# Twelve taps of a depthwise convolution as diagonal products, its taps shared anew among four engines, and three output blocks queued behind a norm's mean

## The chip, the cores and the metric

The kernel runs on one core of one Trainium2 chip. The metric is the device time of one execution in microseconds (us). All times on a trace count from the start of the span. Engines are named as on the profile: PE is TensorE's matmuls, PEld its weight loads, DVE is VectorE, ACT ScalarE, POOL GpSimd, SP the queue that issues the DMAs.

## The reference

An encoder of two layers over 512 tokens of width 1024 in float32. The change lies in the mixer of the second layer, which has two branches over one input projection `p = h @ cd_w_in`, then one output projection and a residual:

```
y_c = real(fftn(p[:, :512] in 4 groups of 128 channels, over tokens and channels, ortho))
val, gate = split(p[:, 512:])
u   = val * sigmoid(gate)                               # 512 channels
u   = depthwise_conv(u, conv_w (31 taps), conv_b)       # centred, per channel
y_d = silu(layernorm(u) * ln_g + ln_b)                  # over the 512 channels
x   = x + gate_vector * (concat([y_c, y_d]) @ cd_w_out)
```

Behind it stand an RMS norm with scale and shift, and a gated feed-forward part.

## The kernel before, in words

Activations lie transposed: 128 channels on the partitions, 512 tokens along the row, so 1024 channels are 8 blocks of 128x512. A projection is done block by block (`gemm`): each fp32 weight block is split into a rounded part `whi` (ScalarE, L136) and a rest `wlo` (VectorE, L137), each input into `h` and its rest, and three products of type fp32r (L142 to L144) make one fp32 product. Norm sums and the channel transform of the Fourier branch use plain fp32 products.

The order of each engine's queue is set by a scheduler that ranks instructions by the place in the program and by priorities (`tc.high_priority`); it is fixed when the program is built. Each engine works its queue in that order.

`layer1` is the mixer. It makes eight blocks for the convolution branch (`hps`, 15 zeros on either side), then four for the Fourier branch:

- `channels(u)`: ScalarE copies the block from PSUM to `u` (L1077); VectorE adds and subtracts the block and its mirror image, the halves `eo` (L1042); TensorE multiplies these with the channel table (L1046, tile `m`), ScalarE and VectorE split the result (`vh`, `vl`, L1049, L1050).
- `tokens(g, v)`: TensorE multiplies with the sequence tables, twelve products of 258 columns (tiles `g` and `c`); VectorE puts the two results together into `y` (L1068, L1069), which is split (L161, L162) as input of the output projection.

The convolution has 31 taps for each of four blocks. Block b's taps from `FO[b]` on go to GpSimd (multiplied by ScalarE into a ring of eight `ta` tiles, L1103, and added by GpSimd into `cpa`, L1108), those below to VectorE, one fused multiply and add each into a PSUM bank (`h`, L1114), after a first one by ScalarE (L1111). FO is {0: 6, 1: 31, 2: 22, 3: 2}: 57 taps on VectorE, 63 on GpSimd (60 of them multiplied by ScalarE). L1117 adds the two sums. Then the layer norm: TensorE sums the four accumulators with a matrix of ones (tile `pm`, L1124), VectorE subtracts the mean (L1127), ScalarE squares (L1129), TensorE sums the squares (`pv`, L1130), ScalarE takes logarithm and exponential (L188, L189), VectorE multiplies (L1134), ScalarE applies silu (L1135).

The output projection (`out_proj`) has two halves: part 0 multiplies the four Fourier blocks with half the rows of `cd_w_out` and adds to the residual `x` (L386), part 1 does so with the four convolution blocks. All eight output blocks of part 0 stand ahead of the convolution in the program.

## Time and profile before

| | |
|---|---|
| median of 3 runs | 1523.39 us (1521.78 to 1528.9) |
| profiled execution, own time | 1523.8 us |
| its span | 1522.0 us |
| busy on PE, DVE, ACT, POOL | 1404.5, 1036.9, 688.2, 162.9 us |
| mean granted TensorE clock | 0.944 of full speed |

A busy TensorE is not TensorE at its peak, since matmuls are pipelined; a stretch is read by its waits and by the granted clock. The clock has two levels, 1.2 and 2.4 GHz, shown as 0.5 and 1.0. The mixer of the second layer begins near 980 us with the modulation of its input; its output projection ends at 1144.92 us.

### The profile page before, as it was taken

Reading aid. Unit: us, or ns where it says so; the run is one execution under the profiler, and the core shown is the slowest. Engines: PE = TensorE matmul, PEld = TensorE weight load, DVE = VectorE, ACT = ScalarE, POOL = GpSimd, SP = SyncE. Lnnn points to the kernel's source line nnn. Section 1 sums busy time; section 2 is a strip of 40 time slices with the busy share of each in tenths; the row PEclk is TensorE's granted clock in tenths of the full one; section 3 lists DMA queues with packets and bytes.
Section 4 is the critical chain, followed back from the end, with each engine's and each line's share of the span. In section 5 each row is a group of like instructions: output and inputs, shape, how many; then the busy total and the mean of one; then the engine's idle time right before and its main releaser. Section 6 shows DMA issues by size and latency. Waiting matters only on the chain.

```text
span 1522.0 us, 22368 instructions
## 1 busy us (share of the span) xinstructions
PE 1404.5 (92%) x8422; PEld 1113.8 (73%) x8422; DVE 1036.9 (68%) x2121; ACT 688.2 (45%) x1231; POOL 162.9 (11%) x226
## 2 busy tenths in 40 slices
PE   5988889889998996999999999998979999999997
PEld 3765567666666674788888888886758888888886
DVE  7689876888696864766565784679968654544544
ACT  4455454635545442643233243576555432332343
POOL 1030210102010000000000000069700000000000
PEclk8998789989999996999999999999799999999999
DMA  9221123412243532344544873221123332223221
GB/s 373 85 78 41 47 54 89 133 46 79 85 149 97 186 108 97 109 154 162 184 140 139 280 268 88 98 91 56 49 70 125 111 97 97 94 87 111 94 73 56
DMA packets 76572, 174.29 MB, mean 115 GB/s; under 512 B 28208, under 2 KB 34224, under 8 KB 75440
## 3 DMA queue, kind: packets, MB, share of 16 engines
q1 hardware_dynamic: 76464, 172.87, 35.0%
q8 instruction: 66, 1.08, 0.3%
q14 instruction: 42, 0.34, 0.1%
HBM read 166.02 MB, written 6.82 MB: 114 GB/s over the span
## 4 chain that ended last, share of the span: by engine, by line
PE 75%; DVE 10%; ACT 5%; issue 4%; DMA 3%; POOL 2%; SPq 1%; DVEq 0%; ACTq 0%; POOLq 0%
PE g L142 9%; PE g L144 9%; PE g L143 9%; PE c L142 5%; PE c L143 5%; PE c L144 5%; PE o L142 3%; PE o L144 3%; PE o L143 3%; PE h L144 3%; PE h L143 3%; PE h L142 3%; DVE wlo L137 2%; PE c L731 2%; PE m L613 2%
## 5 line engine op out<-in xcount | busy, mean ns | idle before, releaser
L136 ACT CAST whi<-raw 128x512 fp32r<-128x512 f32 (+1 forms) x402 | 242.3, 608 | 514.0 <-PE g L143 201.9
L137 DVE TENSOR_TENSOR wlo<-raw,whi 128x512 fp32r<-128x512 f32 (+1 forms) x402 | 279.3, 699 | 180.9 <-ACT whi L136 177.5
L142 PE MATMUL g<-h,whi 128*128 128x512 f32 x586 | 240.7, 411 | 14.9 <-ACT h L170 5.2
L144 PE MATMUL g<-h,wlo 128*128 128x512 f32 x586 | 235.4, 402 | 4.4 <-DVE wlo L137 4.4
L143 PE MATMUL g<-h,whi 128*128 128x512 f32 x586 | 236.3, 403 | 2.9 <-DVE h L171 2.9
L142 PEld LDWEIGHTS g<-h,whi 128*128 128x128 f32 x586 | 113.6, 194 | 45.1 <-ACT h L170 6.5
L144 PEld LDWEIGHTS g<-h,wlo 128*128 128x128 f32 x586 | 113.2, 193 | 31.9 <-DVE wlo L137 5.9
L143 PEld LDWEIGHTS g<-h,whi 128*128 128x128 f32 x586 | 113.4, 193 | 28.7 <-DVE h L171 4.1
L142 PE MATMUL c<-h,whi 128*128 128x512 f32 x306 | 121.8, 398 | 4.8 <-ACT h L161 4.8
L143 PE MATMUL c<-h,whi 128*128 128x512 f32 x306 | 121.4, 397 | 0.0
L144 PE MATMUL c<-h,wlo 128*128 128x512 f32 x306 | 121.1, 396 | 0.0
L1108 POOL TENSOR_TENSOR cpa<-cpa,ta 128x512 f32<-128x512 f32 x60 | 87.2, 1465 | 3.2
L142 PEld LDWEIGHTS c<-h,whi 128*128 128x128 f32 x306 | 58.8, 192 | 18.4 <-ACT h L161 5.6
L639 DVE TENSOR_TENSOR tt<-L,xi 128x60 f32<-128x60 f32 (+24 forms) x248 | 56.2, 227 | 21.1 <-DMA L<-nd 15.6
L230 DVE SCALAR_TENSOR_TENSOR ra<-ra,row 128x1024 f32<-128x1024 f32 x56 | 68.0, 1218 | 0.8 <-DMA ra<-ada 0.7
L143 PEld LDWEIGHTS c<-h,whi 128*128 128x128 f32 x306 | 58.9, 192 | 12.0
L144 PEld LDWEIGHTS c<-h,wlo 128*128 128x128 f32 x306 | 58.7, 192 | 12.1
L641 DVE TENSOR_TENSOR xi<-xi,tt 128x60 f32<-128x60 f32 (+24 forms) x248 | 54.4, 219 | 5.4
L1020 POOL MEMSET hp<- 128x15 f32 x4 | 0.4, 112 | 471.9 <-DVE nt L312 471.9
L142 PE MATMUL o<-h,whi 128*128 128x512 f32 x122 | 48.1, 394 | 0.8 <-DVE ot L791 0.8
L1189 POOL TENSOR_TENSOR h<-x,rs 128x256 f32<-128x256 f32 x4 | 3.7, 934 | 416.2 <-ACT rs L301 416.2
L1103 ACT ACTIVATE ta<-hp,cols 128x512 f32<-128x512 f32 x60 | 41.9, 720 | 13.4 <-POOL cpa L1108 12.8
(431 smaller groups left out, 2974.3 us busy)
## 6 DMA issues: line engine op xcount, KB each, us to landing
raw<-ffn_up SPq DMA_DIRECT2D x88, 512.0 KB, 3.4
ra<-ada SPq DMA_DIRECT2D x56, 512.0 KB, 4.1
raw<-ab_in SPq DMA_DIRECT2D x35, 512.0 KB, 3.6
raw<-ffn_down SPq DMA_DIRECT2D x32, 448.0 KB, 3.3
raw<-ada SPq DMA_DIRECT2D x24, 512.0 KB, 4.1
ada<-ada SPq DMA_DIRECT2D x8, 1024.0 KB, 10.7
raw<-ffn_down SPq DMA_DIRECT2D x16, 512.0 KB, 3.5
raw<-cd_in SPq DMA_DIRECT2D x12, 512.0 KB, 3.3
```

The source lines that it names most:

```text
L136: act.copy(hi[:, :n, :], raw[:, k0:k0 + n, :])
L137: dve.tensor_tensor(lo[:, :n, :], raw[:, k0:k0 + n, :], hi[:, :n, :].bitcast(F32), op=ALU.subtract)
L142: pe.matmul(ps, whi, xhi, start=first, stop=False)
L143: pe.matmul(ps, whi, xlo, start=False, stop=False)
L144: pe.matmul(ps, wlo, xhi, start=False, stop=last)
L230: dve.scalar_tensor_tensor(w, w, 1.0, row, op0=ALU.mult, op1=ALU.mult, accum_out=dst)
L613: pe.matmul(ps[hr, c, :], at[hr, c0 + c], ibk[hr, c0 + c].rearrange("p s t -> p (s t)"), start=True, stop=True)
L639: dve.tensor_tensor(tv, Lv[:, j + 1:, j:j + 1].broadcast_to([P, n, m]), xi[:, j:j + 1, :m].broadcast_to([P, n, m]), op=ALU.mult)
L641: dve.tensor_tensor(xi[:, j + 1:, :m], xi[:, j + 1:, :m], tv, op=ALU.add)
L731: pe.matmul(ps[h][:, c, :], W[hr, c0 + c, :], BRS[hr, c0 + c, :], start=True, stop=True)
L1103: act.activation(tp, hps[b][:, i:i + T], AF.Copy, scale=col("dconv_w", i * 4 + b))
L1108: pl.tensor_tensor(pa, pa, tp, op=ALU.add)
```

## The change

Five things change, all in `layer1`:

1. FO becomes {0: 6, 1: 31, 2: 17, 3: 16}. GpSimd has 54 operations (51 taps from ScalarE), VectorE 55 taps.
2. The first twelve taps of block 3 become twelve fp32 products on TensorE into bank `o`: the weights are a diagonal matrix with the tap's 128 coefficients, the moving operand is the shifted row. The diagonals are new data (`dconv_dg`), loaded in three DMAs of 256 KB into two tiles `dg`. The bias of block 3 goes in with its first `ta` tile.
3. `channels` reads one operand of each half `eo` from the PSUM bank; the other still comes from the copy `u`.
4. Output blocks 5 to 7 of part 0 are issued behind the last product of the norm's mean (`pm`); the norm gets a high priority (`FIRM`). The norm sums block 2 last.
5. The accumulators are the tiles `ys[4:]`, and silu works in place.

```diff
-FO = {0: 6, 1: 31, 2: 22, 3: 2}
+FO = {0: 6, 1: 31, 2: 17, 3: 16}
+PT = {3: 12}
...
-    def out_proj(x, y, src, mod, part, norm=None):
-        for o in range(KB if norm is None else norm.nfull):
+    def out_proj(x, y, src, mod, part, norm=None, os=None):
+        for o in os or range(norm.nfull):
...
-                dve.tensor_tensor(eo[:, i], u[:, 1:H + 1], u[:, T - 1:H - 1:-1], op=op)
+                dve.tensor_tensor(eo[:, i], pu[:, 1:H + 1], u[:, T - 1:H - 1:-1], op=op)
...
-        out_proj(x, yy, "cd_out", mods[1, 0][0], 0)
-        accs = []
-        for b in range(4):
-            accs.append(mk(lp, [P, T], f"acc{b}"))
+        out_proj(x, yy, "cd_out", mods[1, 0][0], 0, os=range(5))
+        accs = ys[4:]
...
+                if i == first + 1 and b in PT:
+                    act.activation(tp, hps[b][:, i:i + T], AF.Identity, scale=col("dconv_w", i * 4 + b),
+                                   bias=col("dconv_b", b))
...
         for b in range(4):
-            ps = mps(tag="h")
-            act.activation(ps, hps[b][:, 0:T], AF.Identity, scale=col("dconv_w", b), bias=col("dconv_b", b))
-            for i in range(1, first_of[b]):
+            begun = PT.get(b, 1)
+            ps = mps(tag="o" if b in PT else "h")
+            if b in PT:
+                for i in range(begun):
+                    if i % 4 == 0:
+                        dg = mk(lp, [P, 4, P], "dg", bufs=2)
+                        nc.sync.dma_start(dg, A["dconv_dg"][b, i // 4])
+                    pe.matmul(ps, dg[:, i % 4], hps[b][:, i:i + T], start=(i == 0), stop=(i == begun - 1))
+            else:
+                act.activation(ps, hps[b][:, 0:T], AF.Identity, scale=col("dconv_w", b), bias=col("dconv_b", b))
+            for i in range(begun, first_of[b]):
...
-        order = (1, 2, 0, 3)
+        order = (0, 1, 3, 2)
         pm = mps()
         for b in order:
-            pe.matmul(pm, ones, accs[b], start=(b == order[0]), stop=(b == order[-1]))
+            with tc.high_priority(FIRM):
+                pmm = pe.matmul(pm, ones, accs[b], start=(b == order[0]), stop=(b == order[-1]))
...
+        with tc.issue_after(pmm.ins):
+            out_proj(x, yy, "cd_out", mods[1, 0][0], 0, os=range(5, KB))
```

Outside the mixer and the start of the feed-forward part behind it, the queues of all engines stay as they were. Line numbers grow by 2 up to the mixer's first lines and by more behind. Three places, first before, then after.

TensorE at the last Fourier group (`m_2032` are its channel products, `c_2040` and `g_2041` its sequence products, `g_2038` those of the group ahead):

```order
L144 MATMUL g_2038_9978<-tab1_1977_9719,vl_2018_9893 128x258
L1046 MATMUL m_2032_9958<-csch_1916_9357,eo_2031_9955 128x128 x2
L1053 MATMUL m_2035_9967<-u_2027_9935,csch_1916_9357 128x1
L1046 MATMUL m_2032_9958<-csch_1916_9357,eo_2031_9955 128x128 x2
L1124 MATMUL m_2170_10492<-acc1_2084_10184,ones_4_74 128x512
L142 MATMUL c_2040_9989<-tab0_1974_9713,vh_2033_9963 128x258
L143 MATMUL c_2040_9989<-tabl0_1975_9714,vh_2033_9963 128x258
L142 MATMUL g_2041_9996<-tab1_1977_9719,vh_2033_9963 128x258
```

The same place after the change:

```order
L144 MATMUL g_2038_9978<-tab1_1977_9719,vh_2017_9892 128x258
L145 MATMUL g_2038_9978<-tabl1_1978_9720,vh_2017_9892 128x258
L146 MATMUL g_2038_9978<-tab1_1977_9719,vl_2018_9893 128x258
L1118 MATMUL o_2128_10339<-hp3_1972_9707,dg_2131_10352 128x512 x4
L144 MATMUL c_2040_9989<-tab0_1974_9713,vh_2033_9963 128x258
L145 MATMUL c_2040_9989<-tabl0_1975_9714,vh_2033_9963 128x258
L144 MATMUL g_2041_9996<-tab1_1977_9719,vh_2033_9963 128x258
L145 MATMUL g_2041_9996<-tabl1_1978_9720,vh_2033_9963 128x258
```

The last four diagonal products (`o_2128`) now stand ahead of the last group's sequence products, and the channel products have moved ahead of `g_2038`, out of sight above the rows; the sum of block 1 (`m_2170` before) has gone further back. The other eight products stand earlier, two of them ahead of the second group's channel products.

VectorE at the end of the convolution (L1114 and L1123 are taps, L1117 and L1128 the additions of GpSimd's sums, L1127 and L1140 the norm's subtraction, `x` the residual additions):

```order
L386 SCALAR_TENSOR_TENSOR x6_1292_6209<-c_2078_10149,mod10_12_93,x6_1292_6209 128x512
L137 TENSOR_TENSOR wlo_2209_10638<-raw_2207_10635,whi_2208_10637 128x512
L1114 SCALAR_TENSOR_TENSOR acc2_2085_10185<-hp2_1958_9631,cols_1_69,h_2152_10412 128x512
L386 SCALAR_TENSOR_TENSOR x7_1293_6210<-g_2082_10169,mod10_12_93,x7_1293_6210 128x512
L137 TENSOR_TENSOR wlo_2212_10644<-raw_2210_10641,whi_2211_10643 128x512
L1117 TENSOR_TENSOR acc2_2085_10185<-acc2_2085_10185,cpa_2112_10261 128x512
L1114 SCALAR_TENSOR_TENSOR acc3_2086_10186<-hp3_1972_9707,cols_1_69,h_2153_10435 128x512
L1117 TENSOR_TENSOR acc3_2086_10186<-acc3_2086_10186,cpa_2121_10287 128x512
L1127 SCALAR_TENSOR_TENSOR acc1_2084_10184<-m_2170_10492,acc1_2084_10184 128x512
L1127 SCALAR_TENSOR_TENSOR acc2_2085_10185<-m_2170_10492,acc2_2085_10185 128x512
L1127 SCALAR_TENSOR_TENSOR acc0_2083_10183<-m_2170_10492,acc0_2083_10183 128x512
L1127 SCALAR_TENSOR_TENSOR acc3_2086_10186<-m_2170_10492,acc3_2086_10186 128x512
```

The same place after the change:

```order
L1128 TENSOR_TENSOR y6_1914_9352<-y6_1914_9352,cpa_2096_10197 128x512
L1123 SCALAR_TENSOR_TENSOR y7_1915_9353<-hp3_1972_9707,cols_1_69,o_2128_10339 128x512
L1070 TENSOR_TENSOR y3_1911_9349<-ev_2042_10003,g_2041_9996 128x256
L1071 TENSOR_TENSOR y3_1911_9349<-ev_2042_10003,g_2041_9996 128x256
L1128 TENSOR_TENSOR y7_1915_9353<-y7_1915_9353,cpa_2110_10238 128x512
L164 TENSOR_TENSOR h_2050_10020<-y3_1911_9349,h_2049_10019 128x512
L1140 SCALAR_TENSOR_TENSOR y4_1912_9350<-m_2148_10416,y4_1912_9350 128x512
L1140 SCALAR_TENSOR_TENSOR y5_1913_9351<-m_2148_10416,y5_1913_9351 128x512
L1140 SCALAR_TENSOR_TENSOR y7_1915_9353<-m_2148_10416,y7_1915_9353 128x512
L1140 SCALAR_TENSOR_TENSOR y6_1914_9352<-m_2148_10416,y6_1914_9352 128x512
L388 SCALAR_TENSOR_TENSOR x0_1286_6203<-c_2054_10029,mod10_12_93,x0_1286_6203 128x512
L139 TENSOR_TENSOR wlo_2161_10473<-raw_2159_10470,whi_2160_10472 128x512
```

Before, the eight residual additions and their weight splits stand among the last taps; now all of them stand behind the norm's subtraction. The last `y` of the Fourier branch (L1070, L1071) stands ahead of the last addition.

TensorE in the norm (before `m_2170` is the mean and `m_2171` the sum of squares, then the second half of the output projection begins; after, `m_2149` is the sum of squares, `c_2070` and `g_2158` are output blocks 4 and 5 of part 0):

```order
L144 MATMUL g_2082_10169<-h_2049_10019,wlo_2081_10166 128x512
L1124 MATMUL m_2170_10492<-acc2_2085_10185,ones_4_74 128x512
L1124 MATMUL m_2170_10492<-acc0_2083_10183,ones_4_74 128x512
L1124 MATMUL m_2170_10492<-acc3_2086_10186,ones_4_74 128x512
L1130 MATMUL m_2171_10497<-nsq_2172_10499,ones_4_74 128x512
L1130 MATMUL m_2171_10497<-nsq_2173_10503,ones_4_74 128x512
L1130 MATMUL m_2171_10497<-nsq_2174_10507,ones_4_74 128x512
L1130 MATMUL m_2171_10497<-nsq_2175_10511,ones_4_74 128x512
L142 MATMUL c_2191_10551<-h_2177_10526,whi_2189_10547 128x512
```

The same place after the change:

```order
L146 MATMUL c_2070_10109<-h_2049_10019,wlo_2069_10106 128x512
L1143 MATMUL m_2149_10421<-nsq_2152_10431,ones_4_74 128x512
L144 MATMUL g_2158_10456<-h_2043_10007,whi_2156_10452 128x512
L145 MATMUL g_2158_10456<-h_2044_10008,whi_2156_10452 128x512
L146 MATMUL g_2158_10456<-h_2043_10007,wlo_2157_10453 128x512
L144 MATMUL g_2158_10456<-h_2045_10011,whi_2156_10452 128x512
L145 MATMUL g_2158_10456<-h_2046_10012,whi_2156_10452 128x512
L146 MATMUL g_2158_10456<-h_2045_10011,wlo_2157_10453 128x512
L144 MATMUL g_2158_10456<-h_2047_10015,whi_2156_10452 128x512
L1143 MATMUL m_2149_10421<-nsq_2153_10435,ones_4_74 128x512
```

Before, the norm's eight sums stand alone; now the sums of squares stand among output blocks 4 and 5, and blocks 6 and 7 follow ahead of the second half. The last two products of the mean stand behind three quarters of output blocks 0 to 3.

## Rows read from the trace of the kernel before

**Rows 1.** This is the page's view of the span in 40 equal slices of 38.05 us (the mixer of the second layer and its output projection lie in slices 26 to 31): busy tenths of TensorE and GpSimd, and the granted TensorE clock in tenths.

```profile
PE   5988889889998996999999999998979999999997
POOL 1030210102010000000000000069700000000000
PEclk8998789989999996999999999999799999999999
```

**Rows 2.** This is the view by stretches of time, of the second layer's mixer and output projection. Columns: stretch, its length, busy us (and instructions) of PE, PEld, DVE, ACT and POOL, granted TensorE clock, DMA share, GB/s.

```profile
1042.15:1045.04 2.89, 0.00 (x0) 0.00 (x0) 2.89 (x5) 1.54 (x3) 2.89 (x3) 0.93 0.40 110
1045.04:1051.31 6.27, 6.08 (x18) 5.02 (x19) 6.24 (x7) 4.81 (x10) 6.27 (x5) 0.50 0.19 67
1051.31:1061.42 10.11, 9.90 (x53) 8.16 (x51) 10.07 (x13) 6.98 (x13) 10.03 (x8) 0.99 0.16 52
1061.42:1063.03 1.61, 0.00 (x1) 0.03 (x1) 1.61 (x3) 0.00 (x0) 1.53 (x2) 1.00 0.32 31
1063.03:1082.30 19.27, 15.79 (x56) 12.60 (x57) 19.16 (x27) 12.03 (x23) 18.25 (x14) 0.56 0.13 39
1082.30:1104.83 22.53, 22.53 (x102) 18.18 (x101) 21.11 (x32) 9.27 (x17) 13.86 (x10) 1.00 0.28 76
1104.83:1119.93 15.10, 6.55 (x15) 2.49 (x15) 8.63 (x15) 9.63 (x14) 0.00 (x0) 0.99 0.24 80
1119.93:1123.34 3.41, 3.41 (x9) 2.70 (x9) 2.17 (x4) 2.91 (x5) 0.00 (x0) 0.53 0.00 0
1123.34:1144.92 21.58, 21.58 (x141) 19.71 (x139) 14.54 (x28) 11.52 (x22) 0.00 (x0) 1.00 0.26 84
1144.92:1148.91 3.99, 1.75 (x8) 0.90 (x7) 3.99 (x11) 3.37 (x8) 0.00 (x0) 1.00 0.19 75
```

**Rows 3.** This is the view of who waited for whom, on TensorE from 960 to 1160 us: total us, times, longest.

```profile
PE m L1046 <- DVE eo L1042: 6.2, 5, 2.9
PE c L142 <- ACT h L161: 4.8, 1, 4.8
PE m L1124 <- DVE acc L1117: 2.3, 1, 2.3
```

**Rows 4.** This is the view of instruction groups by line, on VectorE from 1008.9 to 1108.6 us, shapes kept apart: shapes, count | busy us, mean ns | idle before.

```profile
L1114 DVE SCALAR_TENSOR_TENSOR h<-hp,cols,h 128x512 f32<-128x512 f32 x53 | 39.6, 748 | 5.0 <-ACT h L1111 4.3
L137 DVE TENSOR_TENSOR wlo<-raw,whi 128x512 fp32r<-128x512 f32 x27 | 29.5, 1097 | 1.6 <-ACT whi L136 1.5
L1042 DVE TENSOR_TENSOR eo<-u 128x256 f32<-128x256 f32 x8 | 9.7, 1247 | 0.0
L162 DVE TENSOR_TENSOR h<-y,h 128x512 fp32r<-128x512 f32 x4 | 4.7, 1187 | 0.0
L386 DVE SCALAR_TENSOR_TENSOR x<-c,mod,x 128x512 f32<-128x512 f32 x4 | 3.0, 740 | 0.0
L1068 DVE TENSOR_TENSOR y<-ev,g 128x256 f32<-128x256 f32 x3 | 1.2, 412 | 1.2 <-ACT ev L1066 1.2
```

**Rows 5.** This is VectorE in order of time at the end of the convolution and at the norm's subtraction: start, us, instruction, [idle before <- releaser].

```profile
1107.87 0.69 DVE L1117 TENSOR_TENSOR acc<-acc,cpa 128x512 f32<-128x512 f32 x1
1110.04 2.48 DVE L1127 SCALAR_TENSOR_TENSOR acc<-m,acc 128x512 f32<-128x512 f32 x4 [1.48 <-PE m L1124]
```

**Rows 6.** This is ScalarE in order of time in the norm: squares, logarithm, and the first cast of the branch's result.

```profile
1110.77 2.48 ACT L1129 ACTIVATE nsq<-acc 128x512 f32<-128x512 f32 x4 [4.71 <-DVE acc L1127]
1115.19 0.69 ACT L188 ACTIVATE rs<-m,kconst 128x512 f32<-128x512 f32 x1 [0.64 <-PE m L1130]
1119.27 0.60 ACT L161 CAST h<-y 128x512 fp32r<-128x512 f32 x1
```

**Rows 7.** This is TensorE in order of time: sums of accumulators by the matrix of ones (two records for each fp32 product), sums of squares, and the first product of the second half of the output projection.

```profile
1078.67 1.91 PE L1124 MATMUL m<-acc,ones 128*128 128x512 f32 x2
1107.16 2.84 PE L1124 MATMUL m<-acc,ones 128*128 128x512 f32 x6 [2.33 <-DVE acc L1117]
1111.45 3.70 PE L1130 MATMUL m<-nsq,ones 128*128 128x512 f32 x8 [1.45 <-ACT nsq L1129]
1119.93 0.80 PE L142 MATMUL c<-h,whi 128*128 128x512 f32 x1 [4.78 <-ACT h L161]
```

**Rows 8.** This is one VectorE addition of 128x256 with both operands in SBUF, in order of time, with GpSimd idle.

```profile
1138.76 0.42 DVE L290 TENSOR_TENSOR ss<-ss,nsq 128x256 f32<-128x256 f32 x1
```

**Rows 9.** This is GpSimd in order of time: its last additions.

```profile
1041.76 55.10 POOL L1108 TENSOR_TENSOR cpa<-cpa,ta 128x512 f32<-128x512 f32 x37
```

**Rows 10.** This is the view by stretches, as group 2, over 100 us of the feed-forward part.

```profile
800.00:900.00 100.00, 100.00 (x443) 82.81 (x442) 77.39 (x131) 33.34 (x56) 0.00 (x0) 1.00 0.71 246
```

**Rows 11.** This is the view of DMA issues from 1000 to 1110 us: transfer, queue, count, KB each, median us from issue to landing.

```profile
raw<-cd_out SPq DMA_DIRECT2D x16, 256.0 KB, 2.7
```

**Rows 12.** This is the first pair of Fourier halves on VectorE in order of time.

```profile
1044.15 2.24 DVE L1042 TENSOR_TENSOR eo<-u 128x256 f32<-128x256 f32 x2
```

**Rows 13.** This is TensorE in order of time behind the output projection: the first product of the feed-forward part, and the one with which its products go on after two waits.

```profile
1145.93 0.39 PE L150 MATMUL c<-h,whi 128*128 128x256 f32 x1 [1.00 <-ACT h L313]
1148.91 0.39 PE L151 MATMUL c<-h,whi 128*128 128x256 f32 x1
```

More of the change, by code (lines that the diff above doesn't have):

```diff
@@ L1037, in layer1, with channels @@
             tabs.append((hi, lo))
-        def channels(u):
+        def channels(u, pu):
             eo = mk(lp, [P, 2, H], "eo", bufs=2)
             for i, op in enumerate((ALU.add, ALU.subtract)):
-                dve.tensor_tensor(eo[:, i], u[:, 1:H + 1], u[:, T - 1:H - 1:-1], op=op)
+                dve.tensor_tensor(eo[:, i], pu[:, 1:H + 1], u[:, T - 1:H - 1:-1], op=op)
             ps = mps([P, 2, 2, P])
@@ L1100, in layer1 @@
             for i in range(first + 1, 31):
-                if i < first + 1 + AT[b]:
-                    tp = mk(lp, [P, T], "ta", bufs=TAB)
+                tp = mk(lp, [P, T], "ta", bufs=TAB)
+                if i == first + 1 and b in PT:
+                    act.activation(tp, hps[b][:, i:i + T], AF.Identity, scale=col("dconv_w", i * 4 + b),
+                                   bias=col("dconv_b", b))
+                else:
                     act.activation(tp, hps[b][:, i:i + T], AF.Copy, scale=col("dconv_w", i * 4 + b))
-                else:
-                    tp = mk(lp, [P, T], "tp", bufs=2)
-                    pl.tensor_tensor(tp, hps[b][:, i:i + T], col("dconv_w", i * 4 + b).broadcast_to([P, T]),
-                                     op=ALU.mult)
                 pl.tensor_tensor(pa, pa, tp, op=ALU.add)
         for b in range(4):
-            ps = mps(tag="h")
-            act.activation(ps, hps[b][:, 0:T], AF.Identity, scale=col("dconv_w", b), bias=col("dconv_b", b))
-            for i in range(1, first_of[b]):
-                last = i == first_of[b] - 1
+            begun = PT.get(b, 1)
[6 more added lines that the diff above has]
+                    pe.matmul(ps, dg[:, i % 4], hps[b][:, i:i + T], start=(i == 0), stop=(i == begun - 1))
+            else:
+                act.activation(ps, hps[b][:, 0:T], AF.Identity, scale=col("dconv_w", b), bias=col("dconv_b", b))
+            for i in range(begun, first_of[b]):
+                last = i == first_of[b] - 1 and (b in parts or b not in PT)
                 dve.scalar_tensor_tensor(accs[b] if last else ps, hps[b][:, i:i + T], col("dconv_w", i * 4 + b), ps,
                                          op0=ALU.mult, op1=ALU.add)
+            if b in PT and b not in parts:
+                act.activation(accs[b], ps, AF.Identity, bias=col("dconv_b", b))
         for b in parts:
@@ L1119, in layer1 @@
             pass
-        order = (1, 2, 0, 3)
+        order = (0, 1, 3, 2)
         pm = mps()
         for b in order:
-            pe.matmul(pm, ones, accs[b], start=(b == order[0]), stop=(b == order[-1]))
+            with tc.high_priority(FIRM):
+                pmm = pe.matmul(pm, ones, accs[b], start=(b == order[0]), stop=(b == order[-1]))
         pv = mps()
-        for b in order:
-            dve.scalar_tensor_tensor(accs[b], pm, -1.0 / 512, accs[b], op0=ALU.mult, op1=ALU.add)
-            sq = mk(npool, [P, T], "nsq", bufs=3)
-            last = act.activation(sq, accs[b], AF.Square)
-            pe.matmul(pv, ones, sq, start=(b == order[0]), stop=(b == order[-1]))
-        vr = mk(npool, [P, T], "rs")
-        ln_exp(vr, pv, EPS5, 1.0 / 512, last)
-        for b in range(4):
-            dve.tensor_tensor(accs[b], accs[b], vr, op=ALU.mult)
-            act.activation(ys[4 + b], accs[b], AF.Silu, scale=col("dconv_ln_g", b), bias=col("dconv_ln_b", b))
-            say(f"yd{b}", ys[4 + b])
+        with tc.high_priority(FIRM):
+            for b in order:
+                dve.scalar_tensor_tensor(accs[b], pm, -1.0 / 512, accs[b], op0=ALU.mult, op1=ALU.add)
+                sq = mk(npool, [P, T], "nsq", bufs=3)
+                last = act.activation(sq, accs[b], AF.Square)
+                pe.matmul(pv, ones, sq, start=(b == order[0]), stop=(b == order[-1]))
+            vr = mk(npool, [P, T], "rs")
+            ln_exp(vr, pv, EPS5, 1.0 / 512, last)
+            for b in range(4):
+                dve.tensor_tensor(accs[b], accs[b], vr, op=ALU.mult)
+                act.activation(accs[b], accs[b], AF.Silu, scale=col("dconv_ln_g", b), bias=col("dconv_ln_b", b))
+                say(f"yd{b}", accs[b])
+        with tc.issue_after(pmm.ins):
+            out_proj(x, yy, "cd_out", mods[1, 0][0], 0, os=range(5, KB))
         yy = [split(y) for y in ys[4:]]
@@ L1211, in _layout @@
     a["cd_out"] = np.concatenate([wo[:, :, 0:4], wo[:, :, 4:8]], axis=0)
+    dg = np.zeros((4, 32, P, P), np.float32)
+    dg[:, :31, np.arange(P), np.arange(P)] = f("dconv_w").reshape(31, 4, P).transpose(1, 0, 2)
+    a["dconv_dg"] = dg.reshape(4, 8, 4, P, P).transpose(0, 1, 3, 2, 4)
     up = np.stack([blocks(w) for w in f("ffn_w_up")])
```

2 lines of the change are left out of this document (1 added, 1 removed).

## The prediction

> **What bounds the kernel now.** I read the slices first [rows 1]: from slice 17 on TensorE is busy nine tenths or more at nearly full clock, so a stage pays only where it waits or runs at half clock. The exceptions before the last slice are slices 28 and 30 (eight and seven tenths busy) and 29 (clock seven tenths): the mixer of the second layer, where GpSimd is busy as nowhere else.
>
> Then I cut it by TensorE's waits and granted clock [rows 2], from 1042.15, where its queue first stands still, to 1144.92, the last product of the output projection: 102.77 us. Idle: 2.89 + 0.19 + 0.21 + 1.61 + 3.48 + 8.55 = 16.93 us (length less busy time, stretch by stretch). Lost to the 1.2 GHz level, each beginning after a wait: 6.08 x (1 - 0.50) = 3.04, 15.79 x (1 - 0.56) = 6.95 and 3.41 x (1 - 0.53) = 1.60, together 11.6 us. That leaves 74.2 us of work at 2.4 GHz. TensorE does not bound this stage; 28.5 us of it are waits and what they cost in clock.
>
> Then who is waited for [rows 3]: first the Fourier halves `eo` of VectorE (5 waits, 6.2 us), later the last convolution sum and the norm behind it. VectorE is busy almost without a gap from 1042 to 1104 [rows 2]. Its groups [rows 4] show why: 57 taps of 0.75 us, 27 weight splits and eight `eo` halves. What reads two SBUF tensors is slow while GpSimd adds: a half takes 1.25 us, and one with a PSUM operand, on the same shape in the same stretch (`y`), 0.41. So VectorE is the bound up to the last sum, whose addition starts at 1107.87 [rows 5]; then the norm is a bare chain through three engines until 1119.93 [rows 6, 7].
>
> **Part by part.**
>
> Queue of VectorE ahead of the norm's mean, by the order rows of the change and the durations of before [rows 4]: two taps fewer, 2 x 0.75 = 1.5 us; eight halves from PSUM, 9.7 - 8 x 0.41 = 6.4; eight residual additions now behind the norm's subtraction, 8 x 0.74 = 5.9; eight weight splits that move with them, at the undisturbed 0.69 (that of the final addition [rows 5], same form of operation; 1.10 would be the mean beside GpSimd) 5.5; one split of `y`, 1.2. Sum 20.5: the last addition ends at 1108.56 - 20.5 = 1088.1.
>
> The halves need two bounds, since before has no `eo` with a PSUM operand: 0.41 of `y` and 1.25 of `eo` itself. I take 0.41, whose operands are the same kinds, reversed columns included. A 128x256 addition with both operands in SBUF and GpSimd idle took 0.42 us [rows 8], so at this shape and type the place of the operand costs nothing by itself. The Trainium skill speaks against such a read (VectorE: DVE Perf Modes, "Why PSUM operands drop a tier"): a PSUM operand takes the faster modes away and leaves fp32 at the basic rate. The trace agrees in that fp32 shows no faster mode here that could be lost; were one lost and the half doubled, VectorE's queue would be 3.3 us longer.
>
> GpSimd: 9 of its 63 operations leave. The last 37 additions took 55.10 us [rows 9], 1.49 each, so it ends about 13.4 us earlier, near 1083.5: before VectorE needs its sums, so worth nothing by itself. ScalarE's ten taps fewer likewise; it runs ahead of GpSimd by the ring of eight buffers and had waits to spare.
>
> TensorE gets twelve fp32 products of 128x512. The nearest rows are the norm's sums, of the same form [rows 7]: three in 2.84 us, 0.95 each, at 2.4 GHz, and one of 1.91 at 1.2 GHz. Bounds: 11.4 and 22.9 us, for they lie on the queue that becomes the bound. I take 11.4, because in the change's order they fill places where TensorE stood waiting, the first two ahead of the second group's channel products.
>
> The three blocks moved behind the mean: 36 products at 100/443 = 0.226 us [rows 10], 8.1 us, no more work than before. After the mean TensorE still holds 12 products of blocks 0 to 3, block 4 (12), those 36, and the four sums of squares: 60 x 0.226 + 3.8 = 17.4 us. The norm's chain is delayed by standing among them: the last sum of squares comes after 31 products, 7.0 + 3.8 = 10.8 us behind the mean. From Ln's start to the end of the first cast took 1119.87 - 1115.19 = 4.7 us [rows 6], and a weight cast stands among these, 0.6 more: 16.1. That is 1.3 us inside the cover of 17.4, so the second half of the projection starts on a running engine at full clock. Without the cover its price would be the old gap, 8.55 + 1.60 us.
>
> Three loads of diagonals are added on SP. One of 256 KB landed in 2.7 us [rows 11]. The first two are issued ahead of the Fourier tables, long before use. The third stands behind two weight loads that wait for weight splits of VectorE. From the first halves at 1044.15 [rows 12] to the later of these splits VectorE has 16 taps, 6 weight splits, 6 halves and 7 smaller ones: 12.0 + 6.6 + 2.5 + about 5 = 26 us, so the load goes out near 1070 and lands near 1073. TensorE has, from the end of its third Fourier block near 1053 to its last four new products, 24 block products (5.4), 36 sequence products of half the width (4.1), three channel groups with the columns of one fp32 product and a small one each (about 1.3), and eight new ones (7.6): 21 us, so it wants the load near 1074. Cover about 1 us; a late one is a rival.
>
> **Sum.** On TensorE to the projection's end: 74.2 + 11.4 = 85.6 us of work. What stays: the first wait, 2.89 less the 0.7 by which the first half gets shorter (0.41 instead of half of 2.24 [rows 12]), 2.2; the half clock after it, 3.0, since nothing before that wait changes; and about 1.0 for the handovers between groups (those seen in full-clock stretches are 0.2 each [rows 2]). 91.8 us against 102.77: 11.0 us less. After the projection the norm and the modulation follow the same chain as before, 1144.92 to 1148.91 [rows 13]; the changed order puts the first half's sum later in the last block but nothing else in front of it, so I cost this at nothing, 0.3 either way.
>
> The profiled execution took 1523.8 us (span 1522.0), 0.4 above the median of 1523.39; against the median the forecast is **1512.4 us**. A measurement of this kernel tells about 0.5%, 7.6 us, from no change: the border is 1515.8.
>
> **The rivals.**
>
> *The middle stays as it is* (18%). The ring `eo`, channel products, split, sequence products or the third load of diagonals makes TensorE wait again between 1054 and 1080, and it falls to 1.2 GHz, as it did after 1061.42, where a wait of 1.61 us was followed by 19 us at 0.56. That costs the 3.48 + 6.95 us of that stretch: 1523 us, no change. For it: five waits stood there, and the cover of the third load hangs on VectorE. Against it: `eo` leaves VectorE two thirds sooner, and products that need only the convolution's input stand in the queue where the waits were. It decides from a wait of about 1.6 us on. The Trainium skill (TensorE: Matmul & The Clock Gate, "What's actually happening") has the throttled clock as the default state, released by activity; the half-clock stretches here agree, all three behind a wait.
>
> *Products on top of the waits* (7%, the slower side). The products stand in a fixed queue ahead of the last Fourier group, whose `y` VectorE must finish before the last convolution sum. If the waits stay and TensorE takes the products at 1.2 GHz, they cost 22.9 us ahead of the mean, and only the norm's gap, 8.55 + 1.60 us, is filled: 1523.4 + 12.8 = 1536 us. At full clock they would cost 11.4, just over the gap's worth. So it decides by the clock: slower by over 0.5% from about 1.5 us per product. Against it: VectorE has 20 us less to do, and the diagonals are on chip early.
>
> *The norm's chain is not covered* (8%). ScalarE takes weight casts between the squares, whose buffers come free only when TensorE has finished earlier blocks; with the sums among blocks, the second half could start 4 us late and fall to half clock, 1.6 more. That gives up to 1518 us. Against it: every buffer that these casts want is released by products standing ahead of the sums.
>
> *VectorE's halves do not get faster* is no rival of its own: it gives back 6.4 us on VectorE, whose end at 1088.1 lies about 5 us ahead of the mean on TensorE (last part), and 1514 us come out.
>
> **How the numbers follow.** Forecast 67%, its own range 1507 to 1516; if all idle time and half clock vanished, the saving would be 28.5 - 11.4 = 17.1, so 1506 is the floor. Uncovered norm 8%, middle unchanged 18%, products on top 7%. The 80% range runs from 1506 to 1519: the forecast, the uncovered norm, and part of the middle rival. Faster by over 0.5%: 0.67 and half of the uncovered norm, 0.71. Within: 0.22. Slower: 0.07.
>
> **What would show it.** Right: TensorE with no wait above 0.5 us between 1052 and the second half of the projection, clock at 1.00 from about 1052 on; twelve products at 0.95 us; `eo` halves at 0.41; the projection's last product near 1134, so its second half (24.99 us, 23.4 without the half clock) begun near 1110.5 and the mean done 17.4 us earlier, near 1093; GpSimd done near 1084. Wrong: half clock between 1054 and 1080, a wait for the third load of diagonals, or idle time on TensorE between the mean and the second half. The prediction fails as a whole if the projection's last product is less than 6 us earlier than at 1144.92, or if the stretch after it grows by as much as was won.

## The result, and the profile after

| | before | after |
|---|---|---|
| median of 16 runs each | 1525.13 us (1521.78 to 1532.22) | 1516.05 us (1511.28 to 1523.15) |
| ratio after / before | | 0.9941, 95% interval 0.9923 to 0.9958 |
| stage: TensorE's first stand to the projection's last product | 102.77 us | 90.19 us |
| from there to the end of the span | 377.08 us | 379.05 us |

The change wins 9.1 us in the medians (6.4 to 11.7 by the interval of the ratio). The profiled execution of after took 1522.82 us, near the upper end of its sixteen: TensorE's first stand lies at 1051.76 us in it instead of 1042.15, though nothing ahead was changed. In the executions below that point lies anywhere from 1040 to 1054 us, so I compare lengths from it, and times of after less 9.61 with times of before.

Stretches of after, to set against [rows 2] (columns as there; the last two lie behind the projection):

```profile
1051.76:1054.24 2.48, 0.01 (x2) 0.01 (x1) 2.48 (x5) 1.23 (x2) 2.48 (x2) 1.00 0.31 102
1054.24:1058.60 4.36, 4.36 (x17) 3.82 (x18) 4.33 (x6) 3.22 (x6) 4.36 (x5) 0.61 0.39 117
1058.60:1069.39 10.79, 10.79 (x55) 8.61 (x55) 10.76 (x16) 8.34 (x16) 10.79 (x8) 1.00 0.24 55
1069.39:1080.82 11.43, 10.27 (x48) 6.71 (x46) 10.67 (x16) 9.29 (x17) 11.43 (x9) 1.00 0.13 41
1080.82:1083.88 3.06, 2.10 (x17) 1.89 (x17) 3.02 (x7) 1.44 (x4) 2.90 (x3) 1.00 0.61 171
1083.88:1098.00 14.12, 13.10 (x52) 8.80 (x52) 13.98 (x22) 1.35 (x5) 7.12 (x6) 1.00 0.00 0
1098.00:1102.00 4.00, 4.00 (x14) 2.65 (x15) 1.11 (x2) 0.47 (x1) 0.00 (x0) 1.00 0.00 0
1102.00:1118.97 16.97, 16.97 (x68) 12.62 (x68) 14.02 (x23) 12.51 (x20) 0.00 (x0) 1.00 0.35 102
1118.97:1141.95 22.98, 22.98 (x148) 21.05 (x147) 16.87 (x32) 13.10 (x26) 0.00 (x0) 1.00 0.33 111
1141.95:1146.30 4.35, 2.34 (x9) 0.93 (x7) 4.35 (x12) 4.04 (x10) 0.00 (x0) 1.00 0.51 170
1146.30:1152.20 5.90, 5.90 (x36) 5.90 (x37) 5.90 (x16) 3.98 (x9) 0.00 (x0) 0.71 0.00 0
```

Up to the projection's end, idle time fell from 16.93 to 5.6 us (length less busy time) and the loss at the 1.2 GHz level from 11.6 to 1.7 us (4.36 x 0.39). Between the mean (1102.00) and the second half of the projection (1118.97) TensorE does not stand at all, where it stood 1.45 and 4.78 us before [rows 7]. Behind the projection there is a half-clock stretch that the trace of before does not have, 0.71 over 5.90 us.

Who TensorE waits for up to the projection's end (columns as in [rows 3]):

```profile
PE m L1048 <- DVE eo L1044: 2.8, 2, 2.5
PE g L144 <- DVE y L1071: 1.0, 1, 1.0
PE o L1118 <- DMA dg<-dconv_dg: 1.0, 1, 1.0
PE m L1055 <- DVE vl L1052: 0.8, 1, 0.8
```

VectorE and GpSimd, one row for each step of the prediction: halves `eo`, last convolution sum, norm's subtraction, first residual addition, GpSimd's last additions ([rows 4, 5, 9]):

```profile
1053.77 0.74 DVE L1044 TENSOR_TENSOR eo<-c,u 128x256 f32<-128x256 f32 x2
...
1097.74 0.68 DVE L1128 TENSOR_TENSOR y<-y,cpa 128x512 f32<-128x512 f32 x1
...
1102.04 2.48 DVE L1140 SCALAR_TENSOR_TENSOR y<-m,y 128x512 f32<-128x512 f32 x4 [2.84 <-PE m L1136]
1104.44 0.74 DVE L388 SCALAR_TENSOR_TENSOR x<-c,mod,x 128x512 f32<-128x512 f32 x1
...
1051.38 40.02 POOL L1108 TENSOR_TENSOR cpa<-cpa,ta 128x512 f32<-128x512 f32 x28
```

TensorE in order of time: diagonal products (two records each), the two last sums of the mean, the last sum of squares, the first product of the second half ([rows 7]); then ScalarE's logarithm and first cast ([rows 6]):

```profile
1074.47 2.74 PE L1118 MATMUL o<-hp,dg 128*128 128x512 f32 x6
...
1083.88 3.70 PE L1118 MATMUL o<-hp,dg 128*128 128x512 f32 x8 [0.96 <-DMA dg<-dconv_dg]
...
1100.12 1.88 PE L1136 MATMUL m<-y,ones 128*128 128x512 f32 x4
...
1111.53 1.02 PE L1143 MATMUL m<-nsq,ones 128*128 128x512 f32 x2
...
1118.97 0.39 PE L144 MATMUL c<-h,whi 128*128 128x512 f32 x1
...
1112.59 0.69 ACT L190 ACTIVATE rs<-m,kconst 128x512 f32<-128x512 f32 x1 [2.93 <-PE m L1143]
1117.19 0.62 ACT L163 CAST h<-y 128x512 fp32r<-128x512 f32 x1
```

A product costs 0.91 to 0.93 us. The last sum ends 3.6 us before the mean is done (1102.00), and 1.7 us before its last two sums start (1100.12). From the last sum of squares (1112.55) to the second half TensorE still has 6.4 us of block products.

### The profile page after: what moved, and what is told of

It is laid out like the page before. It is cut to its first block, busy times and chain, and to the rows that moved or that the text cites. A ratio compares the mean times of both kernels' runs of the same rounds, so it can differ in the third digit from the quotient of the medians.

```text
span 1521.0 us, 22382 instructions
## 1 busy us (share of the span) xinstructions
PE 1412.9 (93%) x8446; PEld 1117.7 (73%) x8446; DVE 1028.0 (68%) x2119; ACT 682.8 (45%) x1221; POOL 148.3 (10%) x217
## 4 chain that ended last, share of the span: by engine, by line
PE 72%; DVE 14%; ACT 5%; issue 4%; DMA 3%; POOL 2%; SPq 1%; DVEq 0%; POOLq 0%; ACTq 0%
PE g L144 9%; PE g L146 8%; PE g L145 8%; PE c L145 6%; PE c L144 6%; PE c L146 6%; PE o L144 3%; PE o L145 3%; PE o L146 3%; PE h L144 3%; PE h L146 3%; PE h L145 3%; DVE wlo L139 2%; PE c L733 2%; DVE tt L641 1%
## 5 line engine op out<-in xcount | busy, mean ns | idle before, releaser
L1108 POOL TENSOR_TENSOR cpa<-cpa,ta 128x512 f32<-128x512 f32 x51 | 73.5, 1460 | 1.9
L232 DVE SCALAR_TENSOR_TENSOR ra<-ra,row 128x1024 f32<-128x1024 f32 x56 | 67.9, 1218 | 0.0
L643 DVE TENSOR_TENSOR xi<-xi,tt 128x60 f32<-128x60 f32 (+24 forms) x248 | 54.4, 219 | 5.4
L746 ACT COPY X<-c 64x64 f32<-64x64 f32 x56 | 11.7, 208 | 84.0 <-DVE X L745 83.5
L144 PE MATMUL o<-h,whi 128*128 128x512 f32 x122 | 48.1, 394 | 0.8 <-DVE ot L793 0.8
L145 PE MATMUL o<-h,whi 128*128 128x512 f32 x122 | 47.9, 393 | 0.0
L146 PE MATMUL o<-h,wlo 128*128 128x512 f32 x122 | 47.9, 393 | 0.0
## 6 DMA issues: line engine op xcount, KB each, us to landing
ada<-ada SPq DMA_DIRECT2D x8, 1024.0 KB, 10.7
```

The source lines that it names most:

```text
L144: pe.matmul(ps, whi, xhi, start=first, stop=False)
L145: pe.matmul(ps, whi, xlo, start=False, stop=False)
L146: pe.matmul(ps, wlo, xhi, start=False, stop=last)
L232: dve.scalar_tensor_tensor(w, w, 1.0, row, op0=ALU.mult, op1=ALU.mult, accum_out=dst)
L643: dve.tensor_tensor(xi[:, j + 1:, :m], xi[:, j + 1:, :m], tv, op=ALU.add)
L746: act.copy(X[64:128, 1, cn], ps[64:128])
```

## The experiments

Theory **T**: VectorE's last convolution sum bounded the stage before; with it early, TensorE's own work bounds it. **R1**: VectorE's queue is the bound still. **R2**: the gain is the covered norm; products and halves matter little. The results called for **T2** (products and tap shares bring the last sum forward, and the queueing can cover the norm only then) and **T3** (the cover is decided by the work behind the last sum of squares).

All twelve in one table, with before and after, in us from the moment TensorE's queue first stands still (also where an expectation says "from the end of TensorE's first stand"). "Last sum" is VectorE's last addition of a GpSimd sum, "last square" TensorE's last sum of squares, "wait" TensorE's wait for the first cast of the second half, "tail" what lies behind the projection. The stage of after came out as 90.2 and 90.1 in its two traced executions; every other kernel has one. All ratios are to the kernel before, run on the same chip as the kernel in question; "against" names the kernel that the edit starts from.

| kernel | last sum ends | mean done | last square ends | wait | stage | tail |
|---|---|---|---|---|---|---|
| before | 66.4 | 67.9 | 73.0 | 4.78 | 102.8 | 377.1 |
| e1_psum_only | 63.2 | 67.3 | 72.5 | 4.78 | 102.4 | 379.8 |
| e8_queue_only | 63.2 | 67.1 | 79.0 | 4.78 | 109.3 | 378.2 |
| e2_no_products | 60.5 | 64.2 | 75.9 | 4.78 | 105.8 | 378.1 |
| h_none_sq6 | 60.4 | 64.2 | 70.3 | 0 | 98.4 | 378.2 |
| e4_products_twice | 65.5 | 69.4 | 81.8 | 4.78 | 112.2 | 378.1 |
| g5_queue_undone | 46.7 | 53.0 | 67.3 | 4.78 | 98.3 | 378.3 |
| g4_halves_sbuf | 53.4 | 58.6 | 69.1 | 0 | 98.6 | 377.8 |
| g2_gpsimd_load | 54.4 | 56.5 | 68.1 | 4.78 | 98.7 | 378.1 |
| e6_eight | 47.6 | 53.1 | 67.5 | 4.78 | 98.3 | 378.4 |
| h_e6_sq6 | 47.9 | 52.0 | 61.0 | 0 | 89.0 | 378.1 |
| e5_three_tiles | 46.2 | 49.6 | 59.8 | 0 | 89.3 | 377.3 |
| after | 46.6 | 50.2 | 60.8 | 0 | 90.2 | 379.1 |
| after_again | 46.6 | 50.2 | 60.7 | 0 | 90.1 | 379.3 |

**Halves from PSUM alone** (e1_psum_only, against before).

```diff
-dve.tensor_tensor(eo[:, i], u[:, 1:H + 1], u[:, T - 1:H - 1:-1], op=op)
+dve.tensor_tensor(eo[:, i], pu[:, 1:H + 1], u[:, T - 1:H - 1:-1], op=op)
```

> The kernel before with one edit: one operand of each Fourier half `eo` comes from PSUM. Stage = from the end of TensorE's first stand in the mixer of the second layer to the last product of its output projection (102.8 us before, 90.2 after). T (VectorE's queue ahead of the norm's mean bounds the kernel before): a pair of halves falls from 2.24 to 0.8 us or less, the last convolution sum ends about 6 us earlier, the waits for eo shrink, but the norm's gap of 8.6 us stays: stage 95 to 97 us. R2 (the gain of the change is the filled gap of the norm; halves matter little): stage 101 to 103 us, since the halves' gain turns into waiting elsewhere.

Measured: ratio 0.9997 (0.9974 to 1.002), stage 102.4. T failed here; R2's number and its reason came true. TensorE's waits in the stage, and the last three sums of the mean:

```profile
PE m L1124 <- DVE acc L1117: 4.3, 1, 4.3
PE m L1046 <- DVE eo L1042: 3.7, 2, 2.4
PE c L144 <- DVE vl L1050: 3.1, 1, 3.1
PE c L142 <- ACT u L1055: 2.0, 1, 2.0
...
1106.79 5.49 PE L1124 MATMUL m<-acc,ones 128*128 128x512 f32 x6 [4.33 <-DVE acc L1117]
```

The wait for `eo` fell from 6.2 to 3.7 us, but 3.1 for `vl` (1.2 before) and 2.0 for `u` came up: with the halves early, TensorE reaches the next links of the same chain too early, and has nothing else to do there. The clock was 0.54 from 22.7 to 30.2 us. The last sum came 3.2 us earlier, but the mean only 0.6: TensorE waited 4.3 us for that sum instead of 2.3, and its three sums then took 5.49 us, at half clock, instead of 2.84.

**Queueing alone** (e8_queue_only, against before): `out_proj` with `os=range(5)` ahead, the norm at `FIRM`, and

```diff
+with tc.issue_after(pmm.ins):
+    out_proj(x, yy, "cd_out", mods[1, 0][0], 0, os=range(5, KB))
```

> The kernel before with the queueing alone: output blocks 5 to 7 of the first half behind the norm's mean, the norm at high priority; no diagonal products, halves still from SBUF, old tap shares, old order of the four sums. T: the residual additions and weight splits leave VectorE's queue ahead of the mean (some 11 us), but the halves stay dear and GpSimd's last sum ends where it did (near 1097 on the clock of the kernel before), so the mean is done near 1099 to 1101 and the second half of the projection begins 17 us later: stage 97 to 100 us, no idle time between mean and second half. R2 (the filled gap is the gain): stage 90 to 92 us. If VectorE splits and additions only change places: 102 to 103 us.

Measured: ratio 1.0044 (1.0015 to 1.0072), stage 109.3, slower by 6.5 and against every theory. The waits:

```profile
PE m L1125 <- DVE acc L1117: 7.2, 1, 7.2
PE m L1046 <- DVE eo L1042: 6.1, 5, 2.8
PE c L142 <- ACT h L161: 4.8, 1, 4.8
```

The 8.1 us of products were taken from ahead of the mean, where TensorE then stood 7.2 us instead of 2.3. The mean was hardly earlier (67.1 against 67.9). The last square came behind all 36 moved products, 11.9 us after the mean instead of 5.1, so nothing was left to cover the 4.8 us behind it.

**No products** (e2_no_products, against after).

```diff
-FO = {0: 6, 1: 31, 2: 17, 3: 16}
-PT = {3: 12}
+FO = {0: 6, 1: 31, 2: 22, 3: 2}
+PT = {}
```

> The kernel after without the diagonal products: taps shared as before (57 on VectorE, 63 on GpSimd), the other edits kept. T (TensorE's work bounds the stage after the change, and GpSimd would without it): TensorE has 11 us less to do, but GpSimd's nine additions more end about 13 us later, and the mean waits for GpSimd's last sum, some 6 us later than after the change: stage 94 to 97 us, with TensorE idle ahead of the mean. R1 (VectorE's queue is still the bound, two taps and some additions more): stage 91 to 93 us. R2 (the products are mere load, all of the gain is in the queueing and the halves): stage 80 to 86 us.

Measured: ratio 1.0018 (0.9992 to 1.0044), stage 105.8. TensorE had 11 us less to do and the stage was 15.6 us longer than after: the products, with the tap shares that go with them, are more than load. None of the three numbers came. TensorE stood 10.7 us ahead of the mean, and in the places of the products it waited 3.0 us for `vl` and 2.0 for `u`, as in e1. GpSimd ended at 54.2 us instead of 39.6, the mean was done at 64.2, 14 us later than after, where T had said 6. T's reason is not what the trace shows either: GpSimd had ended 5.6 us before VectorE began its last sum. VectorE has five residual additions and five more weight splits ahead of the last taps here, so its queue is what the mean waits for.

**Products twice** (e4_products_twice, against after).

```diff
+pe.matmul(ps, dg[:, i % 4], hps[b][:, i:i + T], start=False, stop=(i == begun - 1))
```

> The kernel after with each of the twelve diagonal products issued twice, so that these taps count double in the output; nothing else differs. T (TensorE bounds the stage): 12 x 0.92 = 11.0 us more, stage 100 to 102 us, sum of block 2 and mean 10 to 11 us later. R1 (VectorE's last sum bounds the mean, and TensorE has time ahead of it): stage 91 to 96 us. If the longer runs of products keep the clock up where it fell at the first wait, up to 2 us less than T says.

Measured: ratio 1.0089 (1.0056 to 1.0123), stage 112.2, 22 us more where 11.0 were added, outside all numbers named. Of the 22 us 10.3 are work, 6.9 idle time and 4.9 half clock (split as in the section on the result). So the added products cost about what was expected; the rest came since the order changed with them: the last ones sank behind the blocks, and VectorE's last taps behind additions that wait for blocks:

```profile
1103.38 1.02 PE L1119 MATMUL o<-hp,dg 128*128 128x512 f32 x2
...
1103.58 0.75 DVE L388 SCALAR_TENSOR_TENSOR x<-c,mod,x 128x512 f32<-128x512 f32 x1 [3.97 <-PE c L146]
1104.25 0.68 DVE L139 TENSOR_TENSOR wlo<-raw,whi 128x512 fp32r<-128x512 f32 x1
1104.85 2.33 DVE L1124 SCALAR_TENSOR_TENSOR o<-hp,cols,o 128x512 f32<-128x512 f32 x3
```

**Each other part undone.** Queueing (g5_queue_undone, against after):

```diff
-out_proj(x, yy, "cd_out", mods[1, 0][0], 0, os=range(5))
+out_proj(x, yy, "cd_out", mods[1, 0][0], 0, os=range(KB))
...
-with tc.issue_after(pmm.ins):
-    out_proj(x, yy, "cd_out", mods[1, 0][0], 0, os=range(5, KB))
```

(and `high_priority(FIRM)` of the norm is `high_priority(0)`).

> The kernel after with the queueing undone: all eight output blocks of the first half ahead of the norm in the program, the norm without its priority; products, tap shares and halves as after. On VectorE the last convolution sum stands where it stood, so its end should stay at 46 to 48 us from the start of the stage (46.6 after). T2 (products and tap shares bring the last sum forward, the queueing then covers the norm): the sums of squares come behind all blocks, near 65 us, the norm's chain is bare again for 5 to 8 us, some half clock behind it: stage 95 to 99 us (90.2 after, 102.8 before). R2 (the queueing is all of the gain): 101 to 103 us. R3 (the queueing is worth nothing): 90 to 92 us.

Measured: ratio 0.9952 (0.9931 to 0.9973), stage 98.3, 8.1 more than after, as T2 said. The last sum stayed at 46.7 us. Stretches from the last square to the projection's end (PE, PEld, DVE, ACT, POOL, clock, DMA share, GB/s):

```profile
1111.22:1116.00 4.78, 0.00 (x1) 0.00 (x0) 2.52 (x5) 4.68 (x7) 0.00 (x0) 0.88 0.14 56
1116.00:1124.00 8.00, 8.00 (x24) 6.34 (x24) 2.57 (x4) 2.92 (x5) 0.00 (x0) 0.65 0.00 0
```

An uncovered norm costs 4.78 us and 2.8 of half clock behind it (8.00 x 0.35).

Halves from SBUF again (g4_halves_sbuf, against after):

```diff
-dve.tensor_tensor(eo[:, i], pu[:, 1:H + 1], u[:, T - 1:H - 1:-1], op=op)
+dve.tensor_tensor(eo[:, i], u[:, 1:H + 1], u[:, T - 1:H - 1:-1], op=op)
```

> The kernel after with the halves `eo` read from SBUF again, all else as after. A pair of halves goes back from 0.74 to about 2.2 us, 6 us on VectorE's queue in all. T2 with VectorE's queue as the bound of the mean: last convolution sum at 50 to 53 us instead of 46.6, waits for eo again between the Fourier groups, stage 93 to 97 us. TensorE as the bound (VectorE has waits to spare): stage 90 to 92 us.

Measured: ratio 0.9962 (0.9939 to 0.9985), stage 98.6, 8.4 more. The last sum moved by 6.8 us, the mean by 8.4; the norm stayed covered. Neither number came, and VectorE's last sum is not what holds the mean back: it ends at 53.4 us, and the last two sums of the mean, which TensorE works in its order, start at 56.0. What grew lies ahead of them, from the first stand to the mean (1102.72; PE busy, clock, DMA share, GB/s):

```profile
1044.12:1046.93 2.81, 0.00 (x1) 1.00 0.40 90
1046.93:1064.91 17.98, 16.96 (x71) 0.81 0.19 58
1064.91:1080.00 15.09, 13.12 (x46) 0.77 0.20 57
1080.00:1102.72 22.72, 20.68 (x83) 0.92 0.02 6
```

Idle time up to the mean is 7.8 us instead of 5.6 (waits for `eo`, `vl` and the last `y`), and half clock costs 7.9 us instead of 1.7: together the 8.4 us.

GpSimd loaded again (g2_gpsimd_load, against after):

```diff
+if b == 3 and 17 < i < 27:
+    tp = mk(lp, [P, T], "ta", bufs=TAB)
+    act.activation(tp, hps[b][:, i:i + T], AF.Copy, scale=col("dconv_w", i * 4 + b))
+    pl.tensor_tensor(pa, pa, tp, op=ALU.add)
```

> The kernel after with nine further additions on GpSimd (and nine multiplications by ScalarE), which add nine taps of block 3 a second time into the output; GpSimd then has 63 operations as before the change. T2 (the products pay by relieving GpSimd): GpSimd ends near 53 us instead of 39.6, the last convolution sum near 55, the mean near 58, and the second half of the projection begins 6 to 7 us later: stage 95 to 99 us. R1 (only VectorE's queue counts; the prediction priced GpSimd's relief at nothing): stage 90 to 92 us.

Measured: ratio 0.9972 (0.9949 to 0.9996), stage 98.7. GpSimd ended at 53.3 us, the last sum 1.1 us later, the mean at 56.5; the last square came behind all block products, and the 4.78 us were back. T2 holds, R1 does not.

**Eight products** (e6_eight: `PT = {3: 8}`, `FO[3] = 12`).

> The kernel after with eight products instead of twelve; GpSimd takes the four taps, and two loads of diagonals are left. TensorE has 3.7 us less to do, GpSimd ends some 6 us later (near 45 us). T2 with TensorE as the bound of the stage: 86 to 88 us (90.2 after). T2 with GpSimd's end counting as soon as it passes the last taps: last sum near 48, stage 90 to 93 us. If the changed places of the sums among the blocks on TensorE undo the cover of the norm: 94 us or more.

Measured: ratio 0.9957 (0.9935 to 0.9979), stage 98.3: the last case named. The last sum was at 47.6 us, but the last square stands behind all block products of the first half.

```profile
PE c L144 <- ACT h L163: 4.8, 1, 4.8
PE c L144 <- ACT u L1057: 3.0, 1, 3.0
```

The four products that were left out had stood in the place of the second wait.

**Where the last square stands** (h_e6_sq6 against e6_eight, h_none_sq6 against e2_no_products, the same edit).

```diff
 with tc.issue_after(pmm.ins):
-    out_proj(x, yy, "cd_out", mods[1, 0][0], 0, os=range(5, KB))
+    out_proj(x, yy, "cd_out", mods[1, 0][0], 0, os=range(5, 6))
+with tc.issue_after(pvm.ins):
+    out_proj(x, yy, "cd_out", mods[1, 0][0], 0, os=range(6, KB))
```

(`pvm` is the last product of the squares' sum.)

> The kernel with eight products, and output blocks 6 and 7 issued behind the last sum of squares instead of behind the mean; nothing else differs from it (98.3 us of stage, with the second half of the projection waiting 4.78 us for its first cast and half clock behind that). T3 (what decides is how much TensorE holds behind the last sum of squares, against 4.78 us of norm chain): 24 block products, 5.4 us, now stand there, the wait of 4.78 us goes and the half clock behind it: stage 90 to 92 us, as with twelve products. T2 (the number of products or GpSimd's end is what costs): 96 to 99 us as it was.

> The kernel without products, and output blocks 6 and 7 issued behind the last sum of squares instead of behind the mean (without that: 105.8 us of stage, mean done at 64.2, a wait of 10.7 us ahead of the mean and one of 4.78 behind the squares). T3: the wait behind the squares goes with its half clock, 6 to 8 us, the wait ahead of the mean stays, since VectorE and GpSimd are as late: stage 98 to 101 us; the 8 to 10 us that are left to the kernel after (90.2) are then what the twelve products bring. R2 (with the queueing done well the products bring nothing): 90 to 93 us.

Measured: stages 89.0 and 98.4, so 9.3 and 7.5 us less by this edit alone; ratios 0.9913 (0.9881 to 0.9946) and 0.9968 (0.9946 to 0.9991). T3 holds twice: the 4.78 us went both times, with the half clock behind them (7.5 of the 9.3 us, 6.5 of the 7.5; in the first 1.5 more are half clock ahead of the mean). With the norm covered in both, no products (98.4) against twelve (90.2) prices products, tap shares and the order that comes with them at 8.2 us. Eight, with blocks 6 and 7 placed so, do no worse than twelve as built (89.0 against 90.2): 3.7 us of work less, against a wait of 3.0 that twelve do not have and 1.5 more of half clock. Twelve with blocks 6 and 7 placed so were not run.

**Third load** (e5_three_tiles, against after).

```diff
-dg = mk(lp, [P, 4, P], "dg", bufs=2)
+dg = mk(lp, [P, 4, P], "dg", bufs=3)
```

> The kernel after with three tiles for the diagonals instead of two, so that the third load goes out without waiting for products to release a tile. The wait of 0.96 us for it goes. T (nothing else bounds that place): stage 89 to 89.5 us (90.2 after). R1 (the last convolution sum of VectorE, 1.7 us ahead of the mean's last sums, and the wait for `y` take the wait's place): 89.8 to 90.5 us.

Measured: ratio 0.99 (0.9875 to 0.9926), stage 89.3. The 0.96 us went, and the stage is 0.9 shorter, T's number. All three loads now go out together, at 992.6 to 993.6 us. Not only this wait changed: the one of 1.02 us for `y` went too, and one of 0.78 for `vl` came. In after it was not the tile, as the expectation has it, that came last: the first four products had ended at 1076.35, and the third load went out at 1080.84, right behind a weight load (1080.45) that had waited for a weight split of VectorE (to 1080.43). The median of e5, 1513.29 us, lies 2.9 below that of after_again; the intervals of the two overlap. It and h_e6_sq6 are the shortest versions by the trace (stage and tail 466.6 and 467.1, after 469.2).

**After, once more** (unchanged).

> The kernel after once more, unchanged, on the same chip as the three others. Every theory: stage 90.2 us, ratio to the kernel before 0.992 to 0.996. What is left open by the first comparison is what lies behind the projection: if the 2 us more of the first pair (377.1 us before, 379.1 after) belong to the change, 379 us again; if they are the spread of executions (377.8 to 379.8 us in the eight kernels so far), a value anywhere among those.

Measured: ratio 0.9932 (0.9905 to 0.9959), stage 90.1, tail 379.3. The 2 us came again in a second execution of after. That they belong to the changed order behind the projection is not shown. Six microseconds from 4 us behind it, in after_again, e5_three_tiles, before and e1_psum_only (PE busy, clock, DMA share, GB/s):

```profile
1138.06:1144.06 6.00, 5.65 (x34) 0.72 0.00 0
...
1147.20:1153.20 6.00, 5.65 (x45) 1.00 0.00 0
...
1148.92:1154.92 6.00, 6.00 (x49) 1.00 0.00 0
...
1151.33:1157.33 6.00, 6.00 (x30) 0.53 0.00 0
```

In each pair the busy time is the same and the clock is not. The queues of e1_psum_only behind the projection are those of before but for a few like products of TensorE that change places, and its tail is the longest of all, 379.8 us. Half clock stood just behind the projection in nine of the fourteen executions: both of after, and the seven experiments in which TensorE waits there as it does in before (1.00, 0.69 and 0.3 to 0.5 us). Before itself, e5, g4, h_e6 and h_none have none. Why it came in some and not in others is open.

## Why the prediction was right

Forecast 1512.4 us, 11.0 less; measured 9.1 less by the first medians, 10.6 by the traces (12.6 won, 2.0 given back). The median of 1516.05 us lies at the upper edge of the forecast's own range (1507 to 1516); 1.7 of the 3.6 us between are in the kernel before, whose median was 1523.39 in three runs and is 1525.13 in sixteen. Point by point, times of after less 9.61:

- *VectorE's last addition at 1088.1*: 1088.8. The halves took 0.41 us beside a busy GpSimd, as taken, not 1.25. The Trainium skill (SBUF — State Buffer, "SBUF: two separate sides") has an operation with two SBUF inputs blocked while GpSimd holds the ports that the two share; the rows agree: 1.25 us with both inputs in SBUF, before and again in g4, and 0.41 with one in PSUM.
- *GpSimd's end near 1083.5, worth nothing by itself*: 1081.8, and the second half was wrong. It ends 7 us ahead of the last sum; g2 put its end 13.6 us later, past the old place of that sum, and that cost 8.5 us.
- *Twelve products, 11.4 us*: 11.0. Some of it costs nothing in truth, because it stands where TensorE waited; with four of them gone a wait of 3.0 us took the place of 3.7 us of work.
- *Three blocks cover the norm, 17.4 against 16.1 us*: 17.0 against 15.8. Right, and as thin as forecast: 6.4 us stand behind the last square, and 4.78 are needed.
- *Third load wanted near 1074, about 1 us of cover*: it was 0.96 us late, which was named as a rival's trigger. It went out at 1071.2 (forecast near 1070) behind the weight split that the prediction names, landed at 1074.2 (1073) and was wanted at 1073.3 (1074). TensorE was at 2.4 GHz before and behind that wait, so the middle did not stay as it was.
- *The sum, 91.8*: 90.2. Waits left are 5.6 us (forecast 3.2), half clock 1.7 (3.0), and the rest 82.9 us (85.6). The same sum leaves 73.1 and 72.2 us in the two kernels without products, so the products brought 9.8 to 10.7 us, and the other edits took 1 to 2 off the 74.2 of before. That the total came so close is in part luck: the misses of -2.7, +2.4, -1.3 and +2.0 us (work, waits, half clock, tail) nearly cancel.
- *Tail at nothing, 0.3 either way*: 2.0, outside its bounds. Up to the product with which the feed-forward part goes on it is 4.35 us instead of 3.99, with a wait of 1.33 us for VectorE's `h`; the other 1.7 us are the half clock behind it (5.90 x 0.29). The first half's sums now stand at the end of the last block (1141.01 and 1141.80), but the half clock also comes without that order, as e1 and six others show, so its cause is open.
- *Halves that do not get faster, 1514 us*: g4 gave back 8.4 us of stage, not some 2. The 5 us that I put between VectorE's end and the mean were counted to the mean's end; in after the last sum ends only 1.7 us before the mean's last two sums start. But that is not where the 8.4 us arose: in g4 the last sum still ends 2.6 us ahead of them. The waits at the Fourier groups came back, 2.2 us of idle time and 6.2 of half clock, and the prediction had priced VectorE's end alone.
- *What would show it*: the projection's last product at 1132.3 (forecast 1134), its second half begun at 1109.4 (1110.5), the mean done at 1092.4 (1093), the clock at 1.00 from 1049 on (1052). Not met: "no wait above 0.5 us" (0.84, 0.96 and 1.02 us are left). One sign of being wrong, the wait for the third load, did come, without half clock behind it.

So the forecast held with its mechanism, while its account by parts would have been wrong: the VectorE relief that it put at 20.5 us brings nothing by halves alone, and 6.5 us of loss by queueing alone. Undone one at a time, halves, queueing and GpSimd's relief each give back about 8 of 12.6 us of the stage, by one traced execution each. The whole times show less of it: ratios of 0.9962, 0.9952 and 0.9972 against 0.9941 and 0.9932 for after, so 2 to 6 us, each ratio with an interval of 3 to 4 us to either side, where stage and tail of the traces give 7.1 to 7.6. That each part matters is shown by the waits that came back; the size of 8 us rests on the traces.

## What to carry to other kernels

When several engines take turns at ending last, price a change by undoing each part from the whole, not by adding the parts: here three parts of a gain of 12.6 us were each worth about 8 by the traces, and two of them alone nothing or less. A wait for a chain is filled by independent work placed in it, better than by a faster link, which here only moved the wait to the next link. Count the work that stands behind the last instruction of a chain, not the work behind its first.
